# First weight block in three transfers, nine dummy products, and a new order of the steps up to attention

## The chip, the cores and the metric

The kernel runs on one core of a Trainium2 chip. The metric is the device time of one execution in microseconds (us), as the median of several runs; beside it stands one profiled execution, from which every duration below is taken. TensorE (PE) does the matrix products and PEld its weight loads, VectorE is DVE, ScalarE is ACT, GpSimd is POOL, and SyncE (SP) issues all the DMAs of this kernel from one queue. "L517" is line 517 of the kernel.

## The reference

One layer of a decoder on x of 512 tokens by 1024 features, float32: RMS norm, a token mixer, RMS norm and residual, then a SwiGLU feed-forward layer with its own two norms and residual. The mixer reads one combined input projection and has two groups of heads: four heads of differential attention and eight heads of sparse attention with three branches (compressed, selected, window) mixed by gates.

```python
def reference(x, attn_pre_norm, w_in, ..., ffn_post_norm):
    for l in range(DEPTH):
        h = rms_norm(x, attn_pre_norm[l])
        mix = hybrid_mixer(h, l, w_in[l], ..., w_out[l])
        x = x + rms_norm(mix, attn_post_norm[l])
        h = rms_norm(x, ffn_pre_norm[l])
        f = (jax.nn.silu(h @ w_gate[l]) * (h @ w_up[l])) @ w_down[l]
        x = x + rms_norm(f, ffn_post_norm[l])
    return x
```

## The kernel before, in words

Every operand of a large product is cut into a high part (a reduced-precision copy, on ScalarE) and a low part (what is left over, on VectorE), and each product is made of three: high by high, low by high, high by low.

The kernel is a set of named steps, and the order of the work is written out by hand: `PLAN` (from L46) lists the steps up to the end of attention, `PLAN_NORM` (from L115) those behind it. Each engine runs its own instructions in the order of this list, and SP issues its DMAs in that order too, so a step that waits holds up what stands behind it on the same engine. TensorE has one order for the whole kernel.

The opening computes the first six of sixteen column tiles of the input projection (`FIRST`), block by block of the contraction index k (eight blocks of 128 features):

- `wu` (`warm`, L364) issues dummy products of zeros, `WARM` of them.
- `xL{k}`, `xH{k}`, `xl{k}` load block k of x transposed (256 KB), cut its high part (with the norm's gain, ScalarE, L389) and its low part (VectorE, L393). `xS`, `xA` square and add for the row sums `rs`, from which `rn`, `rb` and `rM` make the scaled rope tables.
- `bL{k}.{h}`, `bh{k}.{h}`, `bl{k}.{h}` load part h of block k of the weights of the six tiles (L503), cut it high (L507) and low (L510). `part_of_block` (L489) says which tiles part h holds. Before, block 1, the first to be used, came in two parts: tile 5 (64 KB) and tiles 0 to 4 (320 KB), the larger first.
- `F{m}.{c}.{k}` is one product of tile m (c = 0 high by high, 1 low weights, 2 low x), 18 for each k. Later tiles have `F{m}.{c}`, eight products in one step.

`fR` applies rope to a half of a pair of tiles; `pA`, `pH`, `pL` join the halves and cut them (pair 0 is the queries of the first two differential heads, pair 1 their keys), and `pW` writes the pair to DRAM. From there `LD` steps load a head's queries (L617) and keys (L624, two issues) in the layout of the scores. `Kp` and the like are the compressed branch, `v0p`, `v1p`, `gp` the values.

Attention: `D0` to `D3` are the differential heads, `N0` to `N7` the sparse ones. For each, `S` is a product of scores (L867, L868), `Q` adds the causal mask, `X` is the row maximum, `E` the exponential, `T`, `H`, `L` turn the result and cut it, `V` multiplies it with the values. `SC` is the compressed branch's scores. Queries have three buffers (`BUFS`), keys two; `N4K0` loads the keys of the second group of sparse heads into one of them, and `N4S01` is the first product to read them.

The feed-forward part uses a scheme of seven products of half blocks (`block.f.n`, L1419) whose operands are sums of halves of the weights and of the activations. `sum_ff` (L1376 and on) makes the weight sums on VectorE, `high_ff` and `low_ff` cut them (L1396, L1404), and `put_high`, `put_low` cut the activation sums (`h3.s3` at L1332, `l3.s3` at L1335: token block 3, sum s3), two of which live in a tile named rope. `block.3.7` is the first to need `l3.s3`; `block.4.1` comes next and needs `high_ff.4.a` and `low_ff.4.a`, made from the gate weights that `load_ff.4.g` brings.

Of the kernel before, what the change touches and what calls it, by code (L numbers as in the profile page):

```python
# [50 lines left out]
F0.2.3 xS1 xA3 bl0.0 xH0 F0.0.0 F2.1.3 F2.2.3 xl0 F4.1.2 bL4.0 F5.2.0 bh4.0 F5.1.3 bl4.0 F1.1.3 F1.2.3 xS0 F3.0.0
F3.1.0 xL4 xH4 F4.1.3 F0.1.0 F0.2.0 F5.0.4 xl4 F2.0.0 F5.0.0 F2.1.0 F5.1.0 F5.2.4 F3.2.0 F4.0.4 F3.0.4 F3.1.4 F4.2.4
bL5.0 xL5 bh5.0 bl5.0 xH5 F4.0.5 F5.0.5 cL xl5 F2.2.0 F4.0.0 F3.2.4 xS2 F3.0.5 cc F5.1.4 xL6 xH6 xL7 F3.1.5 xl6
F4.2.0 xH7 xl7 F1.0.0 F4.1.0 KP1 F1.1.0 F1.2.0 xA2 F2.0.4 F2.1.4 F1.0.4 F0.0.4 F2.2.4 xS5 xS7 rL2 F0.1.4 F0.2.4
bL7.0 bh7.0 F4.2.7 F0.0.5 F0.1.5 F0.2.5 F1.1.4 xA5 F1.2.4 xA7 F1.0.5 F1.1.5 F1.2.5 bl7.0 F5.1.7 xS4 xA4 xS6 xA6
F5.2.5 rL0 F4.1.4 bL6.0 bh6.0 F4.2.6 rL3 xA1 rs F4.2.5 F2.0.5 KW10 bl6.0 F4.1.6 F2.1.5 F5.1.5 F2.2.5 F2.0.6 rn rb
F3.2.5 lL Lv01 F4.0.6 F3.0.6 K20 lM rM3 rM0 F4.1.5 Lv00 rM2 Kt0 F4.0.7 v0h0 F5.2.6 v0l0 F5.1.6 F1.0.6 LW0 W0a F1.1.6
F1.2.6 F0.0.6 F0.1.6 F1.0.7 F1.1.7 F4.1.7 fR4 F5.2.7 F3.1.6 F3.2.6 F5.0.6 F5.0.7 F3.0.7 F3.1.7 fR5 CA F2.1.6 F2.2.6
F2.0.7 F3.2.7 F0.2.6 F0.0.7 F0.1.7 F0.2.7 F2.1.7 v0h1 F2.2.7 F1.2.7 v0p2.0 v0l1 Kh10 v0p1.0 W0b W0d rL1 rM1 fR1
v0p3.0 v0p3.1 W0c v0p2.1 CW KL1 fR0 v0p0.0 v0p0.1 v0p1.1 pA0 pH0 Kl10 KX10 Kp10 pL0 fL10 fh10 fL12 fl10 v0a0 F10.0  # L60
# [5 lines left out]
F15.2 Kl02 KO1 KX03 Kp01 Kp02 D0E01 fR15 fL7 fh7 pA7 KW03 D0E11 Kh03 fl7 D0S11 D0Q11 D0X12 D0E10 pH7 pL7 N0K0 Kl03
fL9 fh9 D0S01 fl9 F7.0 F7.1 F7.2 N0K1 Kp03 KO0 N0LD N0S01 N0S1 fR7 D0E12 pA3 N0S0 KT0 N0Q01 KE0 KG0 D0Q01 D0X02 N0Q1
N0X11 Lg0 fL8 fh8 D0E02 K21 D0R gh0 N0X01 D0g F9.0 N0S02 N0S12 N0E11 fl8 N0Q12 N0X13 D0MX3 LW3 N0E01 D0MX0 D0LE
N0E13 W3b D0MX2 N0Q02 N0X03 N0S11 N0X02 pW7 N0E03 N0E02 F9.1 Lg1 KT1 N0Q11 gl0 N0X12 KE1 N0E12 N0Q0 N0X00 N0X10 KS0
F8.0 KF0 F9.2 fR9 D0MX1 gh1 gl1 F8.1 D1LD1 F8.2 fR8 N0E10 N0R1 N0SC N0CX D0T1 N1LD N1S0 gp3.0 gp1.0 gp1.1 KG1 Lv10  # L70
v1h0 gp3.1 v1l0 gp2.0 Lg2 pA4 pH4 gp0.0 gp0.1 pL4 pH3 pL3 N0CA gh2 gp2.1 gl2 gp2.2 D0H1 Lv11 v1h1 D0L1 v1l1 N0CE
N1S01 D0T0 N1Q01 D0H0 D0L0 N1Q0 gp1.2 gp3.2 N0CS N0E00 N0R0 ga2 gd2 ga1 ga3 gd3 gd1 gp0.2 ga0 gt W3a N0g1 N0g0 N0M02
N1X02 N0CM D1S11 gd0 D1LD0 D1S00 D1S10 D0T2 D0H2 N0M00 D1Q11 D1Q00 D1X00 D1Q10 D1X12 D0L2 N1E02 D1X01 v1p0.0 pW3
v1p0.1 D1E12 D1X10 D1X11 N0M03 v1a0 D1S01 D1E01 D1S02 D1E00 N1X10 N1E10 D1S12 D1Q12 v1d0 D1X13 D1Q01 D1E11 D1Q02
D1X03 N0PH D1E13 N0M01 N0T00 N0H00 D0V0 N1X00 N1E00 D0V1 N0L00 D0V2 D0SQ N1S1 N0M12 D0O3 N0M11 N1SC N1CX D1X02 N0M13
N0M10 N0T10 N0H10 N0PL D1E03 W3c N0L10 LW4 N1S02 D0MS D0N1 D1E10 N1Q02 N1X03 N1Q1 N1X11 D1R N0T02 N0T01 N0H02 N2LD
N2S02 D1E02 N0L02 N1CA N0H01 N1X01 N2SC N2Q02 N2X03 N2CX N0TC W3d N0HC D1g D1MX2 N0L01 N0T11 N0H11 v1p1.0 D1MX3
N1E11 N1E03 D1MX0 v1p1.1 v1a1 v1d1 N1S11 LW6 N2S0 N2CA N2S11 KS1 D1MX1 N2E03 N1Q11 N1CE N1CS N1E01 N1R0 D0N2 N2Q11
N2Q0 N1g0 N1M03 KF1 N2CE N1M02 N0T12 N1M01 N0H12 N2X12 N2E12 N3LD N2X00 N0V00 N1M00 N0V01 N1S12 N2S1 N0L11 N0V02
N1Q12 D0N3 D0N4 N1X12 N1E12 N2X10 D1T1 N0L12 N1X13 D1H1 D1L1 N1E13 N2S01 N2E00 N1R1 N0VC N0V10 N1g1 N1M12 D1T0 N2CS  # L80
N2Q01 N1M13 N2Q1 N2X01 D1T2 N0V11 D1H0 N2S12 N3S02 D1H2 N2E10 N2X02 N2E02 N1CM N2X11 N1PH N1PL D1L0 N0V12 N2Q12
N3Q02 N3X03 N2E01 W4h D1L2 D0RB N1M11 D0ML LW1 N1T02 N1H02 v1p3.0 N2R0 N2X13 N2E11 N2g0 N0O1 N0O2 N2E13 N1T01 N2CM
N2R1 N2g1 N1L02 N1H01 N1L01 N1T00 N2M00 N1H00 D1V0 D1V1 D1V2 D1O3 N1L00 N1TC N1HC N1M10 N3SC N3E03 N1T11 N2M03 pW4
D2LD0 D2S00 N3S01 N3Q01 D2Q00 N3CX N1H11 N3CA N3CE N3S1 D2X01 N3CS N2M11 N3S0 N2PH D1SQ N2M12 N4LD D2E01 W6b N2M02
D2S01 N3X02 N3E02 N1L11 N2M10 N3Q0 N3X00 N3X10 N2M01 D2X00 D2Q01 N3Q1 N3X01 N1T10 N1H10 N1L10 N2M13 N3E01 v1p3.1
# [168 lines left out]
def hybrid_block_kernel(  # L254
# [236 lines left out]

    def block(k, j, h):
        if k not in blk:
            blk[k] = {}
# [4 lines left out]
        return blk[k][j][:, a * P:b * P]

    def load_block(k, h):
        a, b = part_of_block(k, h)
        nc.sync.dma_start(block(k, 0, h).rearrange("p (m c) -> p m c", c=P),  # L503
                          wf[a:b, :, k * P:(k + 1) * P].rearrange("m p c -> p m c"))
# [1456 lines left out]
```

## Time and profile before

| what | value |
|---|---|
| median of 3 runs | 627.74 us (627.74 to 629.05) |
| profiled execution | 628.53 us, its span 626.7 us |
| TensorE busy | 614.8 us, 98% of the span |
| VectorE busy | 548.8 us, 88% |
| ScalarE busy | 374.6 us, 60% |
| GpSimd busy | 100.3 us, 16% |
| DMA | 98.41 MB, mean 157 GB/s |

The span is the time from the first instruction to the last. Busy time of TensorE includes products whose ends are modelled, so 98% doesn't mean that it runs at its peak all the time: the chain of work that ended last, which the prediction shows, tells where another engine sets the pace. Rows of a timeline give start, duration, engine, line, operation, what is written and read, how many instructions were merged, and in brackets the idle time before them with what ended it.

### The profile page before, as it was taken

To read this page: it belongs to the slowest core of one execution; us is meant where nothing else is said; L and a number is where in the kernel's file an instruction comes from. 1 tells how busy PE (TensorE), PEld (TensorE's weight loads), DVE (VectorE), ACT (ScalarE), POOL (GpSimd) and SP (SyncE) were. 2 spreads that over 40 slices of the span, in tenths; PEclk is the share of its full clock that TensorE was granted. 3 is DMA by queue.
4 is the path that set the end of the run, shared out by engine and by line. 5 is a ranking of instruction groups with operands and counts; after the bars stand their busy time and mean duration, and the time that the engine had idled before them with its cause. 6 is when DMAs were issued, how large, how long until landed. Compare 5 with 4: busy or idle time off the path is not lost.

```text
span 626.7 us, 10975 instructions
## 1 busy us (share of the span) xinstructions
PE 614.8 (98%) x4066; PEld 558.9 (89%) x4066; DVE 548.8 (88%) x967; ACT 374.6 (60%) x783; POOL 100.3 (16%) x151
## 2 busy tenths in 40 slices
...
DMA packets 38181, 98.41 MB, mean 157 GB/s; under 512 B 4208, under 2 KB 11504, under 8 KB 37232
## 3 DMA queue, kind: packets, MB, share of 16 engines
...
q14 instruction: 21, 0.17, 0.1%
...
## 4 chain that ended last, share of the span: by engine, by line
PE 85%; DVE 9%; ACT 3%; DMA 1%; issue 1%; DVEq 0%; ACTq 0%
PE yz L1419 26%; PE acc L1493 14%; PE fm L534 9%; PE fm L517 5%; PE x L1419 4%; PE v L650 4%; PE tr L898 3%; PE avn L1081 3%; PE acc L1641 3%; PE g L650 2%; PE sc L867 2%; PE sc L868 2%; PE mixp L1152 1%; DMA wraw<-in_wg 1%; PE cmp L749 1%; PE av L959 1%
## 5 line engine op out<-in xcount | busy, mean ns | idle before, releaser
L881 ACT ACTIVATE p<-sc,nm 128x384 f32<-128x384 f32 (+3 forms) x96 | 50.3, 529 | 12.8 <-DVE nm L877 11.0
L1419 PE MATMUL yz<-rope,wbh 128*128 128x256 f32 x352 | 49.2, 282 | 1.6 <-DVE rope L1335 1.6
L877 DVE TENSOR_REDUCE nm<-sc 128x1 f32<-128x384 f32 (+3 forms) x96 | 43.1, 482 | 6.5 <-PE sc L873 4.8
L1419 PEld LDWEIGHTS yz<-rope,wbh 128*128 128x128 f32 x352 | 44.9, 188 | 1.8 <-DVE rope L1335 1.8
L1050 POOL TENSOR_TENSOR p<-p,l 128x384 f32<-128x384 f32 (+3 forms) x64 | 44.8, 727 | 0.9
L911 DVE TENSOR_TENSOR ptl<-tr,pth 128x384 fp32r<-128x384 f32 (+1 forms) x60 | 34.7, 595 | 6.9 <-ACT pth L908 6.4
L908 ACT ACTIVATE pth<-tr 128x384 fp32r<-128x384 f32 (+1 forms) x60 | 30.4, 527 | 7.4 <-PE tr L898 6.7
L1404 DVE TENSOR_TENSOR wel<-e,weh 128x1024 fp32r<-128x1024 f32 x22 | 26.8, 1220 | 7.3 <-ACT weh L1396 4.2
L1396 ACT ACTIVATE weh<-e 128x1024 fp32r<-128x1024 f32 x22 | 23.3, 1057 | 14.7 <-DVE e L1378 7.7
L1396 ACT ACTIVATE wbh<-wraw 128x1024 fp32r<-128x1024 f32 x22 | 23.2, 1056 | 13.4 <-DVE wraw L1383 9.2
L898 PE MATMUL tr<-ident,p 128*128 128x128 f32 x200 | 29.8, 274 | 0.8 <-ACT pct L1073 0.5
L1396 ACT ACTIVATE whi<-wraw 128x1024 fp32r<-128x1024 f32 x22 | 23.1, 1055 | 11.4 <-DMA wraw<-in_wg 10.5
L1542 ACT ACTIVATE whi<-wraw 128x1024 fp32r<-128x1024 f32 x20 | 21.1, 1059 | 13.7 <-PE acc L1493 6.3
L1419 PE MATMUL yz<-rope,wbl 128*128 128x256 f32 x176 | 28.1, 282 | 0.0
L1404 DVE TENSOR_TENSOR wbl<-wraw,wbh 128x1024 fp32r<-128x1024 f32 x22 | 26.7, 1218 | 0.8 <-PE yz L1419 0.6
L1404 DVE TENSOR_TENSOR wlo<-wraw,whi 128x1024 fp32r<-128x1024 f32 x22 | 26.8, 1217 | 0.2 <-ACT whi L1396 0.2
L1548 DVE TENSOR_TENSOR wlo<-wraw,whi 128x1024 fp32r<-128x1024 f32 x20 | 24.1, 1219 | 1.5 <-ACT whi L1542 1.5
L1449 ACT ACTIVATE us<-yz 128x512 f32<-128x512 f32 x22 | 13.0, 593 | 19.4 <-PE yz L1419 19.3
L867 PE MATMUL sc<-kst,qst 128*128 128x512 f32 (+3 forms) x64 | 23.0, 370 | 1.3 <-issue 0.8
L898 PEld LDWEIGHTS tr<-ident,p 128*128 128x128 f32 x200 | 22.3, 141 | 1.9 <-issue 0.6
L1419 PEld LDWEIGHTS yz<-rope,wbl 128*128 128x128 f32 x176 | 23.9, 188 | 0.0
L868 PE MATMUL sc<-kst,qst 128*128 128x512 f32 (+3 forms) x64 | 21.6, 343 | 0.0
...
## 6 DMA issues: line engine op xcount, KB each, us to landing
...
qk<-rope SPq DMA_DIRECT2D x7, 1024.0 KB, 5.3
kst<-qk SPq DMA_DIRECT2D x24, 256.0 KB, 4.8
...
qst<-qk SPq DMA_DIRECT2D x16, 256.0 KB, 3.6
```

What stands on the lines that cost most here:

```text
L534: pe.matmul(st["fm", m], fms[m][w][:, k * P:(k + 1) * P], xx[k], start=(c == 0 and k == 0), stop=(c == 2 and k == NK - 1))
L650: pe.matmul(pts[i], xx[k][:, i * P:(i + 1) * P], ws[c][wi][:, off:off + n], start=(m == 0), stop=(m == 3 * NK - 1))
L867: pe.matmul(sv[i], lhs, kk[:, 0, :w], start=(n == 0), stop=False, skip_group_check=True)
L877: dve.tensor_reduce(nm[i], sv[i], AX.X, OP.max, negate=True)
L881: act.activation(pp[i], sv[i], AF.Exp, bias=nm[i], accum_out=hs["l"][:, row, i:i + 1])
L898: pe.transpose(tr[:, n * P:(n + 1) * P], pp[i][:, j * P:(j + 1) * P], ident)
L911: dve.tensor_tensor(part(u, 1), tv[u], f32(part(u, 0)), OP.subtract)
L1050: pool.tensor_tensor(p, p, hs["l"][:, 1 + br, i:i + 1].to_broadcast(list(p.shape)), OP.mult)
L1396: act.activation(t[0], w[src], AF.Copy)
L1404: dve.tensor_tensor(t[1], W[f][PARTS[n][0]], f32(t[0]), OP.subtract)
L1419: pe.matmul(o, W[f][w][wi][:, k * P:(k + 1) * P], hop[h][hi][:, k * HS:(k + 1) * HS], start=(n < 3 and m == 0), stop=(m == 11), skip_group ...
L1493: pe.matmul(acc[t], a[x][:, t * P:(t + 1) * P], b[y], start=(first and n == 0), stop=(last and n == 2))
```

## The change

The first block of weights comes in three parts instead of two, tile 0 (64 KB), tiles 1 and 2 (128 KB), tiles 3 to 5 (192 KB), smallest first. Nine dummy products stand in place of sixteen. The list of steps has a new order from its start up to about the first steps of head N4; the rest of `PLAN` is the same. In `PLAN_NORM` one step, `l3.s3`, moves one place ahead. No computation changes. The hunks, with of the list only its first line, the lines around D0's first scores and those around `N4K0`:

```diff
-WARM = 16
+WARM = 9
...
-wu xL1 gc xH1 xl1 bL1.1 bh1.1 F2.0.1 F4.2.1 F1.0.1 F4.0.1 bl1.1 bL1.0 bh1.0 F5.0.1 F1.1.1 F2.1.1 F2.2.1 bL2.0 bh2.0
...
+wu xL1 gc bL1.0 xH1 xl1 bL1.1 bh1.0 F0.0.1 bl1.0 F0.1.1 F0.2.1 bh1.1 bl1.1 F2.0.1 bL1.2 bh1.2 F2.1.1 bl1.2 F2.2.1
+F1.0.1 F1.1.1 F1.2.1 xS1 bL2.0 F4.0.1 F4.2.1 bh2.0 bl2.0 F4.1.1 F3.0.1 F5.2.1 F3.1.1 F3.2.1 F5.0.1 F5.1.1 xL2 xH2
...
-KW00 fL14 Kh13 Kl13 F13.0 F13.1 F13.2 fh14 fl14 F14.0 v0d2 KX13 v0d1 Kp13 D0LD1 D0S10 D0LD0 D0S00 D0S12 Kh00 D0S02
...
+Kh10 fl10 v0p0.1 Kl10 Kp10 pH1 fh12 pL1 fR1 pA0 F10.0 pH0 F10.1 F10.2 v0d3 KW11 pL0 fL11 fh11 fl11 fl12 pW1 v0a2
+v0d2 fR10 F11.0 F11.1 pW0 Kh11 D0LD1 KX11 F11.2 F12.0 KX00 Kl11 Kp11 D0S10 D0S11 fR11 D0S12 D0Q12 v0d1 pA5 pH5 D0Q11
...
-W6a N1O1 D2E03 D2S11 N2H11 D2Q10 N1O2 N2L11 D2X11 D2Q11 D2X10 N2T01 N3S11 N3E11 N3S12 W4l N3M02 N2H01 N2HC N4K0
-D2S12 N2T10 D2Q12 D2E10 D2X12 N3Q12 N2L01 N3Q11 N3X12 N2T02 N3PL D2E11 D2X13 v1p2.0 W1h N2H02 N2L02 N2H10 N2L10
...
+D2S11 N4LD N4SC N4CX N2TC D2Q11 D2Q10 N3S11 D2S12 N3M01 N3S12 D2X11 D2E01 N2HC D2X10 N2T10 N3M03 W6b W6a N3PH N3M00
+D2E00 N4K0 N3M02 D2Q12 D2E10 D2X12 N3Q12 N2L01 N3Q11 N3X12 N2T02 N3PL D2E11 D2X13 v1p2.0 W1h N2H02 N2L02 N2H10 N2L10
...
-snap_2.3 sx.1 block.2.3 h3.s3 load_ff.4.u low_ff.3.b block.3.3 sum_x.3 load_ff.4.g high_ff.4.a sum_ff.4.1 l3.s3
+snap_2.3 sx.1 block.2.3 h3.s3 load_ff.4.u low_ff.3.b block.3.3 sum_x.3 load_ff.4.g high_ff.4.a l3.s3 sum_ff.4.1
...
     def part_of_block(k, h):
-        return (0, len(FIRST)) if k != 1 else ((5, 6), (0, 5))[h]
+        return (0, len(FIRST)) if k != 1 else ((0, 1), (1, 3), (3, 6))[h]
...
-        for h in range(2 if k == 1 else 1):
+        for h in range(3 if k == 1 else 1):
```

More of the change, by code (lines that the diff above doesn't have):

```diff
@@ L43 @@
 SCALE = HEAD_DIM ** -0.5
-WARM = 16
+WARM = 9
 FIRST = range(6)
 PLAN = """
-wu xL1 gc xH1 xl1 bL1.1 bh1.1 F2.0.1 F4.2.1 F1.0.1 F4.0.1 bl1.1 bL1.0 bh1.0 F5.0.1 F1.1.1 F2.1.1 F2.2.1 bL2.0 bh2.0
-bl1.0 F5.1.1 F4.1.1 F1.2.1 bl2.0 F0.0.1 F0.1.1 xL2 F0.2.1 xH2 F3.0.1 F5.2.1 F3.1.1 F3.2.1 F3.0.2 xl2 F2.0.2 F2.1.2
-F4.0.2 bL3.0 bh3.0 F5.0.2 F0.0.2 F0.1.2 F1.0.2 F5.1.2 F0.2.2 F3.1.2 F4.2.2 xL3 xH3 F0.0.3 F5.2.2 F3.2.2 F3.0.3
-F1.1.2 F1.2.2 F1.0.3 bL0.0 bh0.0 bl3.0 F3.1.3 F4.0.3 F0.1.3 xL0 xl3 xS3 F5.2.3 F5.0.3 F4.2.3 F3.2.3 F2.2.2 F2.0.3
@@ L51 @@
[L51 to L60, printed above, removed]
@@ L61 @@
-fR2 F10.1 F10.2 fh12 fR3 fL11 fh11 F11.0 fl11 F11.1 pA1 pH1 fl12 v0d0 pL1 F11.2 pW0 KP0 v0a3 KW11 Kh11 KX11 Kl11
-Kp11 F12.0 v0d3 KL0 KX02 fR11 v0a1 fL13 fh13 fl13 v0a2 F12.1 F12.2 KW12 Kh12 Kl12 KX12 Kp12 KW13 pW1 fR10 KX00 pA5
-KW00 fL14 Kh13 Kl13 F13.0 F13.1 F13.2 fh14 fl14 F14.0 v0d2 KX13 v0d1 Kp13 D0LD1 D0S10 D0LD0 D0S00 D0S12 Kh00 D0S02
-fR12 pH5 Kl00 Kp00 pL5 D0Q12 D0Q02 fR13 fL6 fh6 pA6 pH6 fl6 pL6 D0Q00 D0X00 D0E00 KW01 pW5 D0Q10 D0X10 D0X03 F14.1
-D0X11 Kh01 fL15 D0X13 D0X01 F14.2 fR14 Kl01 fh15 D0E03 pW6 fl15 F6.0 F6.1 F6.2 KX01 D0E13 fR6 F15.0 KW02 Kh02 F15.1
@@ L66 @@
[L66 to L85, printed above, removed]
@@ L86 @@
-D0OH N1T12 N1H12 D2S02 N3X11 N1L12 N3E00 v1a3 N3R0 D0OL D2X02 N1V00 v1d3 N1VC N3E10 N1V01 N3g0 N3CM D2E02 N1V02
-N3M01 N2T00 N2H00 N2PL N3M03 N1V10 N1V11 N1V12 D2Q02 N2TC N2L00 N4SC D2LD1 D2X03 D2E00 N3PH N2T11 N4CX D2S10 N3M00
-W6a N1O1 D2E03 D2S11 N2H11 D2Q10 N1O2 N2L11 D2X11 D2Q11 D2X10 N2T01 N3S11 N3E11 N3S12 W4l N3M02 N2H01 N2HC N4K0
-D2S12 N2T10 D2Q12 D2E10 D2X12 N3Q12 N2L01 N3Q11 N3X12 N2T02 N3PL D2E11 D2X13 v1p2.0 W1h N2H02 N2L02 N2H10 N2L10
+wu xL1 gc bL1.0 xH1 xl1 bL1.1 bh1.0 F0.0.1 bl1.0 F0.1.1 F0.2.1 bh1.1 bl1.1 F2.0.1 bL1.2 bh1.2 F2.1.1 bl1.2 F2.2.1
@@ new lines @@
+F1.0.1 F1.1.1 F1.2.1 xS1 bL2.0 F4.0.1 F4.2.1 bh2.0 bl2.0 F4.1.1 F3.0.1 F5.2.1 F3.1.1 F3.2.1 F5.0.1 F5.1.1 xL2 xH2
+F4.0.2 bL3.0 F2.0.2 F0.0.2 F0.1.2 xl2 F1.0.2 F5.1.2 bh3.0 bl3.0 xL3 xH3 F2.1.2 F2.2.2 F5.0.2 F3.0.2 F0.2.2 xl3
+F1.1.2 F4.0.3 F5.2.2 F4.1.2 F3.1.2 F0.0.3 F4.2.2 xL0 xS2 xH0 F4.1.3 F3.2.2 xl0 F5.2.3 F5.0.3 F1.2.2 F5.1.3 F1.0.3
+F1.1.3 F1.2.3 xS3 xA3 bL0.0 bh0.0 bl0.0 F5.2.0 F4.0.0 F4.2.3 F5.0.0 F2.0.3 xS0 F1.0.0 xL4 xH4 xl4 F2.1.3 F2.2.3
+bL4.0 bh4.0 xA2 F0.1.3 F0.2.3 F5.2.4 F2.0.0 F2.1.0 F2.2.0 bl4.0 F5.1.4 xL7 xH7 F5.1.0 F0.0.0 F0.1.0 xL5 xH5 xS4 xl7
@@ new lines @@
+xS7 xl5 xS5 F3.0.3 cL F4.1.4 F3.1.3 F3.2.3 F3.0.0 F3.1.0 F3.2.0 F5.0.4 xL6 xH6 bL5.0 cc lL bh5.0 xl6 xA4 F1.1.0 Lv00
+F4.2.4 F2.0.4 F2.1.4 F4.2.0 F4.2.5 F3.0.4 F3.1.4 xA5 F1.2.0 F3.2.4 F1.0.4 F1.1.4 xS6 xA6 F5.2.5 xA7 xA1 F0.2.0 bl5.0
+rs F3.0.5 rL0 F2.2.4 F2.0.5 F2.1.5 F4.1.0 F2.2.5 rn F5.0.5 F1.2.4 lM rb rL2 F1.0.5 rM2 F1.1.5 F4.0.4 F3.1.5 F3.2.5
+F0.0.4 F0.1.4 F0.2.4 F0.0.5 F0.1.5 F0.2.5 F1.2.5 bL7.0 bh7.0 bL6.0 bh6.0 F4.0.5 F5.0.7 rL3 F5.0.6 F4.1.5 F5.2.6
+bl7.0 fL12 bl6.0 F5.1.5 rM3 v0h0 v0l0 F5.1.7 F5.2.7 F5.1.6 fR5 F4.0.6 F4.2.7 F4.0.7 F4.1.6 F4.1.7 F4.2.6 fR4 CA
@@ new lines @@
+F3.0.6 F3.1.6 F3.2.6 F0.0.6 F0.1.6 F0.2.6 F1.0.6 F1.1.6 F1.2.6 F1.0.7 F1.1.7 K20 Kt0 F2.0.6 F2.1.6 F2.2.6 F2.0.7
+Lv01 rL1 rM1 F3.0.7 F1.2.7 LW0 F2.1.7 F0.0.7 F0.1.7 F0.2.7 CW F2.2.7 F3.1.7 F3.2.7 v0h1 v0l1 v0p1.0 W0b v0p3.0
+v0p3.1 v0a3 W0d fL10 fh10 KP0 rM0 fR3 W0a W0c fR0 v0p0.0 fR2 pA1 KL1 KP1 KX10 v0p1.1 KW10 v0p2.0 v0p2.1 v0a1 KL0
+Kh10 fl10 v0p0.1 Kl10 Kp10 pH1 fh12 pL1 fR1 pA0 F10.0 pH0 F10.1 F10.2 v0d3 KW11 pL0 fL11 fh11 fl11 fl12 pW1 v0a2
+v0d2 fR10 F11.0 F11.1 pW0 Kh11 D0LD1 KX11 F11.2 F12.0 KX00 Kl11 Kp11 D0S10 D0S11 fR11 D0S12 D0Q12 v0d1 pA5 pH5 D0Q11
@@ new lines @@
+pL5 D0X12 KW12 Kh12 Kl12 D0X13 D0Q10 F12.1 F12.2 fL13 fh13 F13.0 fl13 F13.1 F13.2 KW13 Kh13 fR12 D0LD0 Kl13 KX12
+Kp12 fL14 D0S00 KX13 Kp13 fR13 fh14 D0S01 KW00 fl14 pA6 D0E13 F14.0 F14.1 Kh00 F14.2 Kl00 fL6 fh6 D0X10 KX01 D0X11
+pW5 pH6 D0E12 KW01 Kh01 F6.0 fl6 pL6 D0E11 v0a0 Kl01 D0E10 D0R Kp00 Kp01 KX03 K21 fR14 fL15 fh15 fl15 KW02 Kh02 Kl02
+F6.1 pW6 KX02 KO1 F15.0 N0LD F6.2 fR6 KW03 Kh03 Kl03 fL7 F15.1 F15.2 fR15 pA7 N0K1 fh7 Kp02 Kp03 N0S11 D0S02 KO0 KT0
+D0Q02 fl7 N0Q11 N0X12 D0Q01 fL9 fh9 fl9 D0Q00 D0X01 N0E12 D0X00 F7.0 KE0 F7.1 D0E01 D0X02 D0E02 pH7 KG0 F7.2 v0d0
@@ new lines @@
+N0S12 N0K0 N0S02 N0S1 fL8 fh8 N0S0 LW3 D0E00 D0X03 D0E03 D0LE D0g pL7 fl8 N0S01 KT1 KE1 Lg0 gh0 N0Q12 N0X13 pW7
+N0Q02 N0Q01 N0X02 N0E02 W3b N0Q1 N0X11 N0X01 N0Q0 N0X03 gl0 N0E03 Lg1 F9.0 D0MX3 N0E01 fR7 N0E13 D0MX2 N0E11 pA3
+D0MX0 F9.1 W3d KS0 N0X10 N0E10 F9.2 pH3 F8.0 F8.1 F8.2 fR9 KG1 gh1 D0MX1 KF0 D1LD1 D1S12 N1LD N1S0 N1S01 fR8 N0X00
+N0E00 N1SC N1CX pA4 N1CA D0T2 D0H2 gl1 Lg2 D0T1 D0H1 gh2 gl2 pH4 D0T0 D0L1 N0SC N0CX N0CA N0CE pL4 N1Q01 N1X02 D1Q12
+D1X13 N1Q0 N1X00 gp0.0 gp0.1 gp0.2 ga0 gd0 N1X10 D1E13 pL3 LW4 N1CE N1CS gp1.0 D0L2 gp1.1 gp1.2 gp3.0 gp3.1 D0H0
@@ new lines @@
+N0CS N0R0 N1E02 Lv11 W3a N0R1 gp2.0 gp2.1 gp2.2 D0L0 W3c N1E10 gp3.2 D1S11 Lv10 D1LD0 D1S02 ga1 D0V0 gd1 v1h1 v1l1
+v1h0 ga2 v1l0 D1S00 ga3 gt gd3 N0g1 D1S10 N0g0 N0CM N0PH N0M02 N0M00 D0V1 D0V2 D0SQ D0O3 LW1 D1Q02 D1X03 D1E03 N0M11
+D1Q11 gd2 D1X12 D1Q10 D1X10 D1E10 D1Q00 D1X11 D1E11 v1p0.0 v1p0.1 D1E12 v1a0 pW3 N0M03 N0T02 D1X01 D1E01 D1X00 N0M01
+N0T00 KS1 N0PL v1d0 N0H02 N0L02 D1S01 N2LD N2SC D0MS N0H00 D1R N0L00 N2CX LW6 KF1 pW4 D2LD0 D1E00 D1Q01 N0M13 N0M12
+N0M10 N0T10 N0H10 N1S02 D0N1 N1S1 W4h D1X02 N1S12 N0L10 N1E00 N0T01 N0H01 N1Q02 N1X03 N0L01 D1E02 N1Q12 W4l N1Q1
```

10 lines of the change are left out of this document (added).

## The prediction

> **What bounds the kernel.** I read the page first: its span and the chain of work that ended last.
>
> ```profile
> span 626.7 us, 10975 instructions
> PE 85%; DVE 9%; ACT 3%; DMA 1%; issue 1%; DVEq 0%; ACTq 0%
> ```
>
> TensorE carries the end for 85%, VectorE for most of the rest. The profiled execution took 628.53 us (1.83 around its span); the median of the three runs is 627.74. I work out a difference and take it from the median. A measurement of this kernel tells about 0.2% from no change: 1.26 us, so "faster" begins at 626.48.
>
> Next the chain in order of time, which shows where TensorE sets the pace and where it hands over.
>
> ```profile
> 1.22 5.84 PE warm L369 x16
> 7.06 23.62 PE fm L517 x104
> ...
> 252.42 0.60 ACT avt L1089
> ...
> 253.76 0.70 DVE e L1376
> ```
>
> The dummies run straight into the products, 104 of which follow one another in 23.62 us: 0.227 each. A microsecond won ahead of them is won for all that follow in TensorE's order. At 252.4 the chain leaves TensorE through a copy of its last attention result, and VectorE's long stretch starts from there, so a shift passes on into it. Then the list of TensorE's waits, whose longest is
>
> ```profile
> PE yz L1419 <- DVE rope L1335: 1.6, 1, 1.6
> ```
>
> So three places can move the end: the opening, the attention stretch, and that one wait, which the last hunk of the change touches.
>
> **The opening.** The timeline of the first ten microseconds, all engines:
>
> ```profile
> 1.65 1.47 SPq L503 DMA_DIRECT2D wraw<-in_wf  x3
> ...
> 3.95 0.72 ACT L389 ACTIVATE xh<-xraw,gc 128x512 fp32r<-128x512 f32 x1 [1.93 <-DMA gc<-in_gcol]
> ...
> 4.70 0.75 DVE L393 SCALAR_TENSOR_TENSOR xl<-xraw,gc,xh 128x512 fp32r<-128x512 f32 x1 [3.54 <-ACT xh L389]
> 5.04 0.15 PEld L369 LDWEIGHTS <-warm 128*128 128x128 bf16 x1 [0.28 <-issue]
> 5.47 0.15 PEld L369 LDWEIGHTS <-warm 128*128 128x128 bf16 x1 [0.28 <-issue]
> 5.82 0.75 PEld L369 LDWEIGHTS <-warm 128*128 128x128 bf16 x4 [0.21 <-issue]
> 5.87 0.94 ACT L507 ACTIVATE whi<-wraw 128x640 fp32r<-128x640 f32 x2 [1.20 <-DMA wraw<-in_wf]
> 6.64 1.03 DVE L510 TENSOR_TENSOR wlo<-wraw,whi 128x640 fp32r<-128x640 f32 x2 [1.19 <-ACT whi L507]
> ...
> 6.71 0.58 PE L517 MATMUL fm<-xh,whi 128*128 128x512 f32 x1
> ...
> 8.60 0.72 ACT L389 ACTIVATE xh<-xraw,gc 128x512 fp32r<-128x512 f32 x1
> ```
>
> The first product starts at 6.71, right after ScalarE has cut the 320 KB piece that came in at 5.87. TensorE's own queue is then just done with the 16 dummies. Landing times, from the DMA view of the first 30 us, and the shortest high cut of this line (the 128-wide one):
>
> ```profile
> wraw<-in_wf SPq DMA_DIRECT2D x1, 64.0 KB, 4.0
> gc<-in_gcol SPq DMA_DIRECT2D x1, 4.5 KB, 2.7
> ...
> L507 ACT ACTIVATE whi<-wraw x9: 292/847/852, 5.9 to 29.1; 128x768 fp32r<-128x768 f32 x7, 128x640 fp32r<-128x640 f32 x1, 128x128 fp32r<-128x128 f32 x1
> ```
>
> After the change the first weight transfer is 64 KB and is issued at the same 1.65. It lands between 1.65 + 2.7 = 4.35 (what the small transfer just ahead of it takes) and 1.65 + 4.0 = 5.65 (what the 64 KB piece takes now, behind 320 KB). I take 4.35, for it now lies directly behind the small one. ScalarE is busy with xh until 3.95 + 0.72 = 4.67, then cuts for 0.29: weights at 4.96. Dummies start 0.43 apart, so the tenth's place, 5.04, is where nine end: the first product starts at 5.05. It still runs at the dummies' pace, to 5.48. The second needs the low part: xl ends at 5.45, and the 128-wide subtraction is about 0.25 of the 1.03 that the 640- and 128-wide took together, so 5.70. From 5.72 I count 0.227: the weight loads from 5.82 on are 0.2 apart, so the pace doubles about there. The 18 products of this block of k end at 5.72 + 17 x 0.227 = 9.58; before, at 6.71 + 18 x 0.227 = 10.80. **Gain 1.2 us.**
>
> What covers the rest: the last piece (192 KB) ends the same 384 KB that in the trace have landed by about 2.14 + 4.0 = 6.1, the second issue being at a third of the 1.47; its products come tenth, at 5.72 + 8 x 0.227 = 7.5, with a cut of about 0.5 between. The next block of x has its high cut ready at 8.60 + 0.72 = 9.32, a margin of 0.26; the extra transfer delays its issue by 0.49 (1.47 for three) but not the bytes ahead of it. I take 0; without that cover it costs up to 0.23. Bounds of the gain: 64 KB at 5.65 gives cuts at 5.94 and 6.19, an end at 10.1 and a gain of 0.7; no slow product and no gap gives 5.05 + 4.09 = 9.14 and 1.7. The additional cuts on ScalarE and VectorE and the additional issue on SP lie beside this and cost nothing there.
>
> On the pace: the clock row reads 1.00 throughout, yet dummies are 0.43 apart until 5.47 and 0.2 apart from 5.82, some 4.5 us after the first. [...]
>
> **The attention stretch.** The order is new up to about 181 us, where head N4 begins. The waits there:
>
> ```profile
> 178.44 0.30 PE L867 MATMUL sc<-kst,qst 128*128 128x128 f32 x1 [0.43 <-ACT p L881]
> ...
> 180.19 0.40 PE L867 MATMUL sc<-kst,qst 128*128 128x512 f32 x1
> ...
> 180.66 0.39 PE L867 MATMUL sc<-kst,qst 128*128 128x512 f32 x1
> ...
> 186.21 0.41 PE L867 MATMUL sc<-kst,qst 128*128 128x384 f32 x1 [0.79 <-issue]
> ```
>
> ```profile
> SPq L624 <- PE sc L868: 6.2, 1, 6.2
> ```
>
> 180.19 is N3S12, 180.66 is D2S12, 186.21 is N4S01. N4's keys go into the buffer of the first group's keys, last read by N3S12; SP waited 6.2 us for that. From there to N4S01 it takes what the load takes, and TensorE ran out of work 0.79 early. The new order puts D2S12 ahead of N3S12, so 180.66 - 180.19 = 0.47 of cover is gone: **loss 0.47** (0 to 0.5). D2S10 at 178.44 followed the load into the buffer that D2S02 frees; in the new order N4's queries take that buffer, and N4SC follows closely, while D2's second load now stands 53 steps ahead of its first use: one wait for another, 0 (-0.4 to +0.8).
>
> The other load that comes closer is that of head D0, whose first scores move ahead of six groups of eight products (F12.1 to F14.0) and two of Kp.
>
> ```profile
> 50.49 0.68 DVE L565 TENSOR_TENSOR rope<-rope 128x512 fp32r<-128x512 f32 x1
> ```
>
> ```profile
> 64.51 0.95 PE cmp L749 x8
> ...
> 80.11 0.06 PE sc L867
> ...
> 83.26 14.56 PE fm L534 x64
> ```
>
> ```profile
> qk<-rope SPq DMA_DIRECT2D x7, 1024.0 KB, 5.3
> kst<-qk SPq DMA_DIRECT2D x24, 256.0 KB, 4.8
> ```
>
> TensorE reaches D0S10 at 80.11 - 6 x 14.56/8 - 2 x 0.95 - 1.2 = 66.1. Its operands hang on pL0, which ended at 51.17; the new order puts ahead of it on VectorE two rope halves, pA1 and pL1 (two 0.6 steps each, the width of this row without overlap) and two cuts, about 6.4 us, less the 1.2 of the shift: 56.4 at the latest. The row sums, on which its rope tables wait, follow 85 products instead of the 104 above, 4.3 us less; if VectorE fills all of that, 52.1. Add the write's 5.3, three issues of about 0.5 and a landing of 4.8: 63.7 to 68.0. The wait is 0 to 1.9; the middle, 65.9, just misses TensorE, and I put a chance of a wait in at 0.3: **loss 0.3**.
>
> **The swapped step.** l3.s3 goes ahead of sum_ff.4.1 on VectorE. The timelines of VectorE, ScalarE and TensorE there:
>
> ```profile
> 318.09 0.69 DVE L1376 TENSOR_TENSOR e<-wraw 128x512 f32<-128x512 f32 x1 [1.87 <-DMA wraw<-in_wg]
> 318.70 0.68 DVE L1335 TENSOR_TENSOR rope<-s,rope 128x512 fp32r<-128x512 f32 x1
> ...
> 319.90 1.22 DVE L1404 TENSOR_TENSOR wlo<-wraw,whi 128x1024 fp32r<-128x1024 f32 x1
> ```
>
> ```profile
> 315.09 0.62 ACT L1332 ACTIVATE rope<-s 128x512 fp32r<-128x512 f32 x1
> 317.99 1.06 ACT L1396 ACTIVATE whi<-wraw 128x1024 fp32r<-128x1024 f32 x1 [2.28 <-DMA wraw<-in_wg]
> ```
>
> ```profile
> 319.44 0.74 PE L1419 MATMUL yz<-rope,wbh 128*128 128x256 f32 x4 [1.56 <-DVE rope L1335]
> ...
> 320.50 0.63 PE L1419 MATMUL yz<-x11h,whi 128*128 128x256 f32 x4
> ...
> 321.44 0.64 PE L1419 MATMUL yz<-x11h,wlo 128*128 128x256 f32 x4
> ```
>
> VectorE idles 1.87 us for the gate weights, with l3.s3 queued behind though its input was done at 315.71; TensorE waits 1.56 for l3.s3. Swapped, l3.s3 fills the idle time and TensorE goes on at 317.88. What is late next: block 3.7 ends 1.56 earlier, at 318.9, but block 4.1 needs the high cut that ends at 317.99 + 1.06 = 319.05, then after 0.94 the low one, which moves up by l3.s3's 0.6 to end at 320.5; its products at 321.44 then start at 320.5. **Gain 0.9** (0.6, if VectorE leads from there, to 1.56).
>
> **Sum**: -1.2 + 0.47 + 0 + 0.3 - 0.9 = -1.3 us: 627.74 - 1.3 = 626.4 (profiled: 627.2).
>
> **Rivals.** *Slower: D0's keys come late.* With pL0 at its latest the wait is 1.9; if write and load together also take 2.1 more than the medians above, D0S10 waits 4.0 instead of 0.3: 626.4 + 3.7 = 630.1. It decides from a wait of 1.6 on (627.7). For: VectorE has 6.4 us more ahead of pL0. Against: the bracket's middle makes it. Chance 0.17.
>
> *The clock.* If the 0.25 us gap behind the first product restarts the count, the doubled pace comes 4.5 us later: products of 0.43 instead of 0.227 over 4.5 us lose 2.1: 628.5. Against: TensorE is busy 95% of the time before. [...] Chance 0.05.
>
> *Opening and swap at their lower bounds*, 0.7 and 0.6 (the small piece lands late, VectorE leads behind 319): 626.4 + 0.5 + 0.3 = 627.2. For: VectorE is the chain before 319. Chance 0.23.
>
> *The new order is better in attention too*, the waits of 0.43 and 0.79 and my 0.3 for D0 all gone: 626.4 - 1.5 = 624.9. Against: the cover counted above shrinks. Chance 0.13.
>
> **Numbers.** Forecast 0.42, its own range 625.6 to 627.0; it straddles the 626.48, some three fifths below. Faster: 0.25 + 0.13 + 0.10 of the lower-bound case (one bound of the two costs too little to lose it) = 0.48. Slower than 629.0: 0.14 + 0.02 = 0.16. The rest, 0.36, is the same. Range: 624.4 to 629.4 leaves out the far side of the late keys and of the better order.
>
> **What would show it.** Right: a first product near 5.05, the 104 products without a wait, no wait of TensorE on the rope tile near 317, a wait of about 1.2 ahead of N4S01. Wrong: a wait at the first scores near 66, products at 0.43 after 6, or a new wait behind 319.

## The result and the profile after

The kernel after takes 624.43 us (median of four runs, 624.13 to 625.62) beside 628.11 for the kernel before (four runs): a ratio of 0.994, with an interval of 0.9926 to 0.9954. Run again in a later batch (`e_after2` below), it took 624.35 (ratio 0.9934, 0.9913 to 0.9956). It is faster by 3.7 us, where the forecast was 1.3. The profiled execution took 624.13 us, 4.4 less than that of before.

The page of after, its span and the chain of work that ended last:

```profile
span 622.2 us, 10956 instructions
PE 96%; DVE 2%; ACT 1%; issue 0%; DVEq 0%; ACTq 0%
```

Of VectorE's 9% of the chain, 7 have gone to TensorE. The list of TensorE's waits says why; it is now this short:

```profile
PE warm L369 <- DVE warm L366: 1.2, 1, 1.2
PE tr L898 <- DVE p L947: 0.3, 1, 0.3
```

The wait on the rope tile (1.6), the one at the scores (0.8) and two of about half a microsecond that stood in the list of before are not there. The chain and TensorE's timeline give the time at two points that both kernels pass with the same work behind them: the first product of the values and the first of the mixer's output. First the values from the chain of before and of after, then the mixer from their timelines:

```profile
41.13 11.51 PE v L650 x96
```

```profile
40.38 11.51 PE v L650 x96
```

```profile
252.22 0.44 PE L1166 MATMUL mix<-wh,oh 128*128 128x512 f32 x1
```

```profile
249.23 0.44 PE L1166 MATMUL mix<-wh,oh 128*128 128x512 f32 x1
```

So the opening won 41.13 - 40.38 = 0.75, the attention stretch another 252.22 - 249.23 - 0.75 = 2.24, and what is left of the span's 4.5 us, some 1.5, came behind it, at the wait on the rope tile. The forecast had 1.2 won, 0.77 lost and 0.9 won. In the second profile of after the three are 0.9, 1.3 and 1.4.

The opening of after, on all engines:

```profile
4.48 0.79 ACT L507 ACTIVATE whi<-wraw 128x128 fp32r<-128x128 f32 x2
...
4.83 0.84 PE L517 MATMUL fm<-xh,whi 128*128 128x512 f32 x1
...
5.62 0.79 PE L517 MATMUL fm<-xh,wlo 128*128 128x512 f32 x1
6.21 0.63 PE L517 MATMUL fm<-xl,whi 128*128 128x512 f32 x1
6.63 0.61 PE L517 MATMUL fm<-xh,whi 128*128 128x512 f32 x1
7.06 0.42 PE L517 MATMUL fm<-xh,wlo 128*128 128x512 f32 x1
7.32 0.40 PE L517 MATMUL fm<-xl,whi 128*128 128x512 f32 x1
```

The first product starts at 4.83 and the second at 5.62 (forecast: 5.05 and 5.70). But products are still 0.43 apart up to 7.06, and the pace doubles there instead of at 5.7.

Last, the two loads that the waits hung on, from the DMA view around their issues, before and after: the second half of N4's keys, and the gate weights that `sum_ff.4.1` waits for.

```profile
kst<-qk SPq DMA_DIRECT2D x1, 256.0 KB, 4.8
...
wraw<-in_wg SPq DMA_DIRECT2D x1, 512.0 KB, 5.3
```

```profile
kst<-qk SPq DMA_DIRECT2D x1, 256.0 KB, 3.0
...
wraw<-in_wg SPq DMA_DIRECT2D x1, 512.0 KB, 3.9
```

Same loads, same issues around them, and they land 1.8 and 1.4 us sooner after their issue. Nothing in the forecast has that, and the experiments are mostly about it.

### The profile page after: what moved, and what is told of

It is laid out like the page before. It is cut to its first block, busy times and chain, and to the rows that moved or that the text cites. A ratio compares the mean times of both kernels' runs of the same rounds, so it can differ in the third digit from the quotient of the medians.

```text
span 622.2 us, 10956 instructions
## 1 busy us (share of the span) xinstructions
PE 613.7 (99%) x4059; PEld 559.0 (90%) x4059; DVE 548.1 (88%) x968; ACT 374.2 (60%) x784; POOL 99.6 (16%) x151
## 4 chain that ended last, share of the span: by engine, by line
PE 96%; DVE 2%; ACT 1%; issue 0%; DVEq 0%; ACTq 0%
PE yz L1419 30%; PE acc L1493 14%; PE fm L534 9%; PE fm L517 5%; PE mix L1166 5%; PE x L1419 5%; PE v L650 4%; PE tr L898 4%; PE avn L1081 3%; PE acc L1641 3%; PE g L650 2%; PE sc L867 2%; PE sc L868 2%; PE mixp L1152 1%; PE cmp L749 1%; PE av L959 1%
## 5 line engine op out<-in xcount | busy, mean ns | idle before, releaser
L881 ACT ACTIVATE p<-sc,nm 128x512 f32<-128x512 f32 (+3 forms) x96 | 50.4, 529 | 16.5 <-DVE nm L877 16.2
L1050 POOL TENSOR_TENSOR p<-p,l 128x256 f32<-128x256 f32 (+3 forms) x64 | 45.2, 733 | 1.0
```

Source lines behind the costliest of these rows:

```text
L881: act.activation(pp[i], sv[i], AF.Exp, bias=nm[i], accum_out=hs["l"][:, row, i:i + 1])
L1050: pool.tensor_tensor(p, p, hs["l"][:, 1 + br, i:i + 1].to_broadcast(list(p.shape)), OP.mult)
```

## The experiments

All ratios are to the kernel before, run between on the same chip. In the kernels marked with a star all line numbers are one lower.

### One part at a time

The swap alone, `e_swap`:

```diff
-... high_ff.4.a sum_ff.4.1 l3.s3
+... high_ff.4.a l3.s3 sum_ff.4.1
```

> The kernel before with l3.s3 ahead of sum_ff.4.1 and nothing else. By the trace after, the whole wait of 1.56 us on the rope tile is gone and nothing takes its place: -1.5 us, and no wait of TensorE behind block 3.7. By the prediction's term the cuts of the gate weights are late next: -0.9, with a new wait of about 0.6 ahead of block 4.1. If the stretch in which VectorE leads had to be shortened as well before anything could be won (it is so in the trace after, where attention ends 3 us earlier), this alone brings less than 0.6.

Measured: 628.04 us, ratio 0.999 (0.9977 to 1.0003). TensorE's timeline there:

```profile
319.34 0.73 PE L1419 MATMUL yz<-x11h,whi 128*128 128x256 f32 x4 [0.44 <-ACT whi L1396]
...
320.94 0.74 PE L1419 MATMUL yz<-x11h,wlo 128*128 128x256 f32 x4 [0.39 <-DVE wlo L1404]
```

The wait of 1.56 is gone, and the high cut and then the low cut of the gate weights are late in its place, as the prediction named them: 1.56 - 0.83 = 0.73 is won at this place, and the products on the low cut start 0.50 earlier than in the kernel before (320.94 for 321.44). In the time of the whole that isn't told from no change. With the gate weights landing as late as they do here (after 5.5 us), their high and low cuts hold TensorE up, and the swap brought no more.

The opening alone, `e_open`*: three transfers, nine dummies, the first steps in the new order up to the second load of x, everything behind as before:

```diff
-WARM = 16
+WARM = 9
...
-        return (0, len(FIRST)) if k != 1 else ((5, 6), (0, 5))[h]
+        return (0, len(FIRST)) if k != 1 else ((0, 1), (1, 3), (3, 6))[h]
...
-        for h in range(2 if k == 1 else 1):
+        for h in range(3 if k == 1 else 1):
```

> The kernel before with the new opening only: three transfers, nine dummies, the steps of the first block of k in their new order, everything behind in the old order, no swap. By the trace after: the first product near 4.83, a pause behind it, products 0.43 apart until about 7.0, so the values' products start 0.75 us earlier than before, at 40.4, and that reaches the end only as far as the load of N4's keys and VectorE's stretch let it: -0.75. By the prediction's term: the pace doubles at 5.7 and the gain is 1.2.

Measured: 624.5 us, ratio 0.9948 (0.9932 to 0.9964): the gain of the whole change, from the part that was to bring 1.2. In its profile the values' products start 0.85 earlier than before, but the mixer's 1.5 earlier and the products behind the rope tile 2.6 earlier: the wait of 0.79 at N4S01 is gone (one of 0.3 stands at 187.3, behind the last of the four loads of keys that are issued there) and the one on the rope tile is down to 0.4, although not a step was moved there. The gate weights landed after 4.2 us, N4's keys after 3.1.

Run once more beside the kernel after (label `e_openswap`, though nothing is swapped in it):

> The kernel before with the new opening and nine dummies alone, once more, beside the kernel after on the same chip, to tell what the new order and the swap add to it. If they add what the first traces differ by, this is 1.5 to 1.9 us slower than the kernel after; if the fetches have taken away the waits that they were to remove, the two are within 0.4 us.

Measured: 625.5 us, ratio 0.9967 (0.9948 to 0.9985), 1.15 above the kernel after in the same batch and between the two expectations. All 18 runs of this kernel have a median of 625.4, the ten of after 624.4. So by the medians order and swap add about 1 us to the opening, less than its traces differed by at first (the intervals of the batch overlap). The wait on the rope tile in its first profile and in this second one, which is of one of its three longest executions (628.77 us):

```profile
PE yz L1418 <- DVE rope L1334: 0.4, 1, 0.4
```

```profile
PE yz L1418 <- DVE rope L1334: 1.8, 1, 1.8
```

In the second the gate weights landed after 5.5 us, and the last of the four loads of keys, after 6.3, made a wait of 1.1. What the opening wins at these waits is no fixed amount.

The new order alone, `e_attn`*, with the old opening (old transfers, 16 dummies) and without the swap:

> The kernel after with the old opening (two transfers, 16 dummies, the old order of the first 30 steps) and without the swap: only the new order behind. By the trace after: TensorE's waits of 0.6, 0.4 and 0.8 in attention are gone and the attention stretch is 2.2 us shorter, -2.2 us. By the prediction's terms it is slower by 0.8: a wait of 1.2 ahead of N4S01 and one at D0's first scores near 67.

Measured: 627.14 us, ratio 0.9986 (0.9971 to 1.0). The prediction had it lose 0.8, and it does not. By the medians it wins 1.0, less than half of the 2.2 that the first trace let expect, and the interval reaches to no change. The waits of before on the copy `pct` (0.5) and at D2S10 (0.4) are gone; at N4S01 there is one again:

```profile
185.29 0.41 PE L866 MATMUL sc<-kst,qst 128*128 128x384 f32 x1 [1.03 <-ACT p L880]
```

The second half of N4's keys landed after 5.0 us here, at 185.2, right ahead of it, while ScalarE had long been done. The order of the steps is that of after; there the same load took 3.0.

### Why the same loads land sooner: first theory

One more DMA in the opening moves every later one to the next of eight semaphores that SP's DMAs use in turn: in the traces of before and of after each of its 239 and 240 DMAs takes the one that follows in the row 100, 101, 103, 104, 105, 107, 108, 109. The expectations take these for eight queues; the DMA view has all of SP's transfers in one queue, q1. If a load's place in that turn decides how it is served, that explains both loads. `e_split1` is the kernel before with one load that nobody waits for (37.6 us) in two halves, `e_splitlate` the same at 222.7 us. The helper that loads weights, shortened:

```diff
-        nc.sync.dma_start(raw[:, :w], src)
+        n = 2 if len(calls) in SPLIT else 1; calls.append(n)
+        [nc.sync.dma_start(raw[:, j * w // n:(j + 1) * w // n], src[:, j * w // n:(j + 1) * w // n]) for j in range(n)]
```

> The kernel before, with one weight load (the output weights at 37.6 us, which nothing waits for) issued as two halves, and nothing else: from there on every DMA goes to the next of SP's eight queues. Theory of the queues' turn: the second half of N4's keys goes to the queue of semaphore 101 and lands about 3.0 us after its issue (4.78 before), the wait of 0.79 ahead of N4S01 goes; the gate weights behind 312 land after about 4.1 us (5.33 before), and the wait of 1.56 on the rope tile falls to about 0.4: together -1.9 us, without any change of the opening. Theory of the order alone: the same landings and waits as before, 0 us.

Measured: 628.59 us, ratio 1.0006 (0.9992 to 1.0019). N4's keys moved on in the turn and landed after 4.9 all the same; the gate weights after 5.1.

> The kernel before, with the gate weights' load at 222.7 us issued as two halves: the turn of the queues moves by one behind N4's keys, but ahead of the gate weights at 312.6. Theory of the queues' turn: the wait of 0.79 ahead of N4S01 stays, the gate weights land after about 4.1 us and the wait of 1.56 on the rope tile falls to about 0.4: -1.1 us. Theory of the order alone: 0.

Measured: 628.04 us, ratio 1.0002 (0.9988 to 1.0016); gate weights after 5.5.

The other way round, `e_wrap` is the kernel after with seven such splits, so that the turn stands as before:

> The kernel after with seven weight loads between 98 and 141 us issued as two halves each, which turns the eight queues back to where they stood in the kernel before. Theory of the queues' turn: the second half of N4's keys lands 4.8 us after its issue, a wait of about 0.9 stands ahead of N4S01 again, the gate weights land after about 5.2 us and VectorE's low cut is late behind 317: 1.5 to 2 us slower than the kernel after, some 626.2. Theory of the order alone: within 0.3 us of the kernel after.

Measured: 624.8 us, ratio 0.9946 (0.9927 to 0.9964). Landings 3.0 and 4.2, no wait at either place (its profile has waits of 0.8 at 72 us and 0.7 at 551 us that the kernel after has not). The theory of the turn falls on all three.

`e_open2` leaves the number of DMAs as before: tile 0, then tiles 1 to 5.

```diff
+        return (0, len(FIRST)) if k != 1 else ((0, 1), (1, 6))[h]
```

> The kernel before with the new opening in two transfers (tile 0, then tiles 1 to 5) and nine dummies: as many DMAs as before, the small piece first. Theory of the queues' turn: the first product near 4.83, some 0.5 us of the opening's 0.85 won (the larger second transfer lands later), the waits at N4S01 and on the rope tile as before: -0.5 us, not the -3.6 of the three transfers. Theory of the order alone: the earlier start by itself makes the waits behind go, -3 us or more.

Measured: 628.87 us, ratio 1.0005 (0.9987 to 1.0024). The larger second piece is late: TensorE waits 0.60 and 0.35 in the opening, and the values start 0.5 later than before. Yet the profiled execution had a span of 624.2, the loads landing after 3.7 and 3.8 us. In nine of its twelve runs the granted clock was 0.995 or less, and they took 627.6 to 631.9; the other three took 626.0 to 626.4. So its time says little on the landings; its profile says that they can be early with two transfers, too, and at the old places in the turn.

### Second theory: TensorE's instruction fetches

What e_open, e_open2, e_wrap and after share, and no other kernel up to here, is nine dummies. The page of before counts TensorE's instructions, and the DMA view has two queues for instructions beside the one for data:

```profile
PE 614.8 (98%) x4066; PEld 558.9 (89%) x4066; DVE 548.8 (88%) x967; ACT 374.6 (60%) x783; POOL 100.3 (16%) x151
```

```profile
q1 hardware_dynamic: 38128, 97.72, 47.6%
q8 instruction: 32, 0.52, 0.3%
q14 instruction: 21, 0.17, 0.1%
```

4066 products and 4066 weight loads are 8132 instructions; the 32 transfers of q8, of 16 KB each, make one for 254 of them. From the start of one of these transfers to the next, TensorE starts 252 products and weight loads on average, in before and in after alike (199 to 294 in before, 220 to 282 in after). So I take these for TensorE's own fetches, tied to places in its program, which is an estimate from these counts; seven dummies fewer (14 instructions) then move each of them to a later step. In the kernel before one starts at 313.9, 1.3 us after the issue of the gate weights, while their bytes move; in after none starts until they have nearly landed (the DMA view in 313.9 to 314.0 of before, and in 312.9 to 313.0 of after, 3.3 us after the issue; the stretches from the issue up to there have none of q8; the share counts the transfer's whole time, 1.9 and 0.9 us, so it can pass 100%):

```profile
q8 instruction: 1, 0.02, 118.0%
```

```profile
q8 instruction: 1, 0.02, 59.2%
```

The transfers of q14, mostly of 8 KB, don't go with the landings: three late loads have one that starts in their first microsecond (e_attn, e_a16, e_a7), and so have three early ones (after, e_n3first, second after).

Three kernels change the number of instructions and as little else as can be. `e_a7` is the kernel after with seven dummies more, of one column and one weight, in TensorE's pause behind its first product:

```diff
+    op("wu2", lambda: [pe.matmul(st["warm"][:1, :1], st["wb"][:, :1], st["wb"][:, :1], start=True, stop=True) for j in range(7)])
...
-... F0.0.1 bl1.0 ...
+... F0.0.1 wu2 bl1.0 ...
```

> The kernel after, with seven dummy products of one column and one weight (14 instructions of TensorE, hidden in its pause behind the first product): nothing else is changed. Theory of the fetches: TensorE's 16 KB instruction fetches come 14 instructions earlier in the program again, as in the kernel before; the one near 311 falls into the load of the gate weights (start 1.3 to 2.4 us after the issue, not 3.3), which lands after 5 us or more instead of 3.9, and the second half of N4's keys may land after 4.7 instead of 3.0: waits of about 1 us each, 1 to 2 us slower than the kernel after, 625.5 to 626.5. Theory that the opening's earlier start or the order itself made the waits go: within 0.4 us of the kernel after.

Measured: 625.27 us, ratio 0.9957 (0.9937 to 0.9976). The median is 0.8 above the kernel after, with intervals that overlap; the profile is plain. Its opening is 0.3 ahead of after's, and at the end its span is 2.2 longer (624.4). The fetch is at 312.7, 2.9 us after the issue, and the load lands after

```profile
wraw<-in_wg SPq DMA_DIRECT2D x1, 512.0 KB, 6.0
```

with TensorE waiting 0.9 for the high cut and 0.4 for the low one behind it. N4's keys were little touched (3.4).

`e_b9` is the kernel before with `WARM = 9` and nothing else:

> The kernel before with nine dummies instead of sixteen and nothing else: TensorE idles about 1.6 us ahead of its first product, which starts near 6.7 as before. Theory of the fetches: 14 instructions fewer, so the gate weights land after about 4 us and the second half of N4's keys after about 3: the waits of 0.79 and 1.56 shrink to about 0 and 0.4, some 1.9 us faster than the kernel before where the clock doubles in time. Theory of the earlier start: nothing starts earlier, so no gain; up to 0.5 slower if the pause delays the doubling of the clock by one period of 3.4 us.

Measured: 627.82 us, ratio 0.9985 (0.9966 to 1.0004); the profiled span is 624.9, 1.8 less than before. Gate weights after 4.2, N4's keys after 3.6, the rope wait 0.4: the landings came as the theory has them. The median didn't follow: the twelve runs spread from 625.5 to 629.6. TensorE now pauses for 1.55 ahead of its first product, and waits 0.9 for another part of the keys; what of the spread is due to which isn't settled.

`e_b36` goes the other way: the kernel before with more dummies, 10 of the usual size and 26 of one column, and the opening as it was.

> The kernel before with 36 dummies instead of sixteen, 10 of the usual size and 26 of one column and one weight: the opening, the transfers and the order stay, the first product comes about where it was (6.7, at most 0.7 later), but TensorE has 40 instructions more ahead of everything, so its fetches come 40 instructions earlier in the program. Theory of the fetches: the one near 313.9 then comes about 2.4 us earlier against the load of the gate weights, before its bytes move, and the load lands after about 4.2 us instead of 5.3, with the wait on the rope tile down to 0.5: 1 us or more faster than the kernel before for more work. Theory that fewer dummies help by themselves, or that only an earlier start of the products helps: no gain, up to 0.7 slower.

Measured: 626.4 us, ratio 0.9978 (0.9964 to 0.9993): faster for more instructions. Its waits, and its two loads:

```profile
PE yz L1419 <- DVE rope L1335: 0.7, 1, 0.7
PE tr L898 <- ACT pct L1073: 0.5, 1, 0.5
PE sc L867 <- ACT p L881: 0.4, 1, 0.4
```

```profile
kst<-qk SPq DMA_DIRECT2D x1, 256.0 KB, 3.0
...
wraw<-in_wg SPq DMA_DIRECT2D x1, 512.0 KB, 4.4
```

The fetch starts 0.25 ahead of the load's issue; the wait at N4S01 is gone, the one on the rope tile halved, and the two waits that belong to the order stay. (In this execution the first product also came 0.6 earlier; that much of the 1.6 us need not come from the landings.) All 16 profiles for the gate weights:

| kernels | fetch starts, us after the load's issue | load lands after, us |
|---|---|---|
| before, e_swap, e_attn, e_split1, e_splitlate, e_a16, e_a7 | 1.3, 2.4, 1.9, 1.9, 1.8, 1.2, 2.9 | 5.3, 5.5, 5.0, 5.1, 5.5, 4.7, 6.0 |
| e_open2 | 2.8 | 3.8 |
| after, e_open, e_wrap, e_b9, e_n3first, second after | 3.3, 3.5, 3.4, 3.3, 3.8, 4.1 | 3.9, 4.2, 4.2, 4.2, 4.3, 4.6 |
| e_b36 | -0.25 | 4.4 |
| e_open, second profile | 3.4 | 5.5 |

Fourteen of sixteen fit: a fetch that starts between 1.2 and 2.9 us after the issue goes with a landing after 4.7 us or more, any other start with 4.6 or less. The two bounds are read off these same profiles. e_open2 is at the border, and the second profile of e_open has a late load with its fetch where the early ones have it. The packets show where the time goes. A load ends in sixteen packets of 4 bytes. In before, fifteen of them lie before 316.6, 4.0 us after the issue, and the last at 317.5; in after all sixteen lie before 313.3, 3.7 us after it. So in before one share of sixteen, 1.05 us behind the fifteenth, holds the whole load up. It is so in five more late profiles, the second of e_open among them.

For the second half of N4's keys the fit is looser. In the old order the four profiles with 16 dummies land after 4.7 to 4.9 us, with a fetch that starts 2.2 to 2.5 us after the issue; the other five land after 3.0 to 3.7, with a fetch at 2.6 or none in the load. In the new order six land after 3.0 to 3.5, with a fetch at 2.5 to 3.1 or none, but e_attn after 5.0 with a fetch at 2.9, which doesn't fit. The third of the four loads of keys issued there fits in all sixteen profiles: it lands after 4.7 to 5.0 us in the ten where a fetch starts 1.5 to 2.4 us after its issue, after among them, and after 3.9 to 4.4 in the six where none does. The fourth took 6.1 and 6.3 us in two profiles that have no fetch in it (e_b9 and the second of e_open). So fetches are not the only thing that delays.

### Two checks on the rest

`e_a16` is the kernel after with `WARM = 16`:

> The kernel after with sixteen dummies: the dummies hold the first product back until about 6.7 to 7.1, so the direct gain of the opening is lost (0.8 to 1.2), and by the theory of the fetches the instructions stand as in the kernel before, with the late landings and waits of about 1 us each: 626 to 627. If the fetches do nothing: 625.3.

Measured: 625.8 us, ratio 0.9966 (0.9951 to 0.9981), 1.4 above the kernel after and between the two expectations. Gate weights after 4.7, a wait of 0.33 there, none at N4S01.

`e_n3first`* is the kernel after with N3S12 and D2S12 in their old order:

```diff
-... N3S11 D2S12 N3M01 N3S12 ...
+... N3S11 N3S12 N3M01 D2S12 ...
```

> The kernel after with N3S12 and D2S12 exchanged again, so N3S12 first as in the kernel before. By the prediction's term, cover of 0.47 comes back: a load of N4's keys that is issued 0.47 earlier against its first reader. By the trace after, N4's keys took the other buffer there, the one that D2S12 frees, and waited for whichever of the two products is first: the load is issued at the same distance, about 4.4 us ahead of N4S01, and the time is that of the kernel after within 0.2 us.

Measured: 624.06 us, ratio 0.9932 (0.9908 to 0.9956), which isn't told from after. SP issued the load behind the first of the two products in either order, and N4S01 ran without a wait. The load goes to the buffer of whichever group is read for the last time first.

The kernel after, again:

> The kernel after itself, once more. A second profile: the clock's doubling at another place between 4.0 and 7.4 and with it 18 products of the first block that end between 9.5 and 10.2; the gate weights landing after 4.3 us or less, no wait of TensorE from the second block of k on, 624.4 us.

Measured: 624.35 us, ratio 0.9934 (0.9913 to 0.9956). The time came as expected; the gate weights landed after 4.6 us and not 4.3, and there are two new waits of TensorE, 0.3 and 0.2.

## Why the prediction was right or wrong

The direction was right, and the size came from somewhere else. Point by point:

**Opening, forecast 1.2.** The first two products came where the working put them (4.83 and 5.62 for 5.05 and 5.70), and the extra issue, cuts and the next block of x cost nothing, as it said. The doubled pace did not come 4.5 us after the first dummy: it came at 7.06 in this execution, so the 18 products won 0.75. That the first product still runs at the dummies' pace, 0.2 in the sum, was an estimate from the dummies of before, 0.43 apart up to 5.47: in after it did, 0.84 us from 4.83 with the clock's step at 7.1, and in e_wrap, with the step at 4.3, it took 0.49 from 4.88. Over the seven profiles with the new opening and nine dummies of the usual size the values start at 39.91 on average, over the five with the old one at 41.21: 1.3. The term was right on average, where the clock's step comes at 6.0 and 6.2 and not at 7.1; the trace of one execution could not give it.

**What rode on the opening, forecast nothing.** This is the step that failed. The prediction costed the nine dummies by their time alone and took the two long waits, 0.79 at N4S01 and 1.56 on the rope tile, as fixed by the order of the steps ("From there to N4S01 it takes what the load takes"). But the same load took 3.0 to 5.0 us (the second half of N4's keys) and 3.8 to 6.0 us (the gate weights) over these profiles, and in 14 of 16 the gate weights landed late or early by where TensorE's instruction fetch fell, and so by the number of dummies. With the opening alone the total fell by 2.7 (18 runs). The earlier start accounts for 1.3 of it; the other 1.4 is a difference, and the first profile of e_open has it at those two waits. e_b36, e_b9 and e_a7 move the fetches both ways and the landings with them; that part is shown for the gate weights. For the second half of N4's keys it is likely and not shown (e_attn doesn't fit). How a fetch holds a load up, and on which of the DMA engines, stays open.

**N4S01, forecast a loss of 0.47.** Wrong in its mechanism: the cover wasn't lost, since N4's keys took the other buffer. SP issued the load at 178.82 in after, behind D2S12 and ahead of the end of N3S12, and in e_n3first as close behind N3S12. The forecast wait of "about 1.2" did turn up in e_attn, 1.03, for the late landing and not for the order.

**D2S10, forecast 0 (a wait for a wait).** The wait of 0.43 went and none came, and the 0.5 on `pct` that the prediction left out went too. **D0's first scores, forecast 0.3.** TensorE reached them at 66.36 (forecast 66.1) with no wait. The rival of late keys, at 0.17, did not happen. Alone the new order wins 1.0 by the medians (e_attn, the interval reaching to no change), where the prediction had a loss of 0.77. The rival "better in attention too", at 0.13, names the waits that are gone in after. Its sum left the loss of 0.47 standing: with the whole wait of 1.26 at N4S01 gone it is 626.4 - 0.43 - 1.26 - 0.3 = 624.4 and not 624.9. That this meets the measured 624.43 is luck: the wait at N4S01 stood in e_attn, in the same order of steps, and the wait on the rope tile gave more than the forecast had.

**Swap, forecast 0.9.** Right in its mechanism, the next late things being the two cuts it named, and 0.73 at the place. In the time of the whole, alone, it isn't told from no change (0.1 by the medians). In after the place won about 1.5, because the gate weights came sooner (3.9 us after the issue for 5.3), which makes the cuts of `high_ff.4.a` early as well.

**The rival of the clock.** The gap behind the first product, whose successor starts 0.79 us after it where the spacing is 0.43, did not restart the 4.5 us. By the rival the pace would have doubled 4.5 us later than forecast, near 10; it doubled at 7.06, and the nineteenth product starts at 10.27.
